# The first 128 columns of each weight chunk, 16 bytes ahead of the rest

## The chip, the core and the metric

The kernel runs on one core of one Trainium2 chip. The metric is the time of one execution on the device, in microseconds (us); lower is better. The core has a matrix engine (TensorE; PE in the profile, and PEld for its weight loads), VectorE (DVE), ScalarE (ACT), GpSimd (POOL) and SyncE (SP), which here issues the transfers from the chip's memory.

## What is computed

The reference runs two transformer blocks on 256 positions of width 1024, all in fp32, batch 1. The first adds 16 meta tokens in front (272 positions), then runs a gated feed-forward layer, a mixer with two kinds of attention, and a second feed-forward layer; the second block runs a convolution and a retention mixer, cross attention to 256 memory rows, and a squared-ReLU layer. Nearly all work is products of an activation with a weight matrix that is read once:

```python
def swiglu(h, w_in, w_out):
    gu = h @ w_in
    gate, up = jnp.split(gu, 2, axis=-1)
    return (jax.nn.silu(gate) * up) @ w_out

def first_block(...):
    h = jnp.concatenate([pad, meta, x], axis=1)
    for l in range(DEPTH):
        h = h + 0.5 * swiglu(rms_norm(h, ffn1_norm[l]), ffn1_w_in[l], ffn1_w_out[l])
        h = h + token_mixer(rms_norm(h, mix_norm[l]), ...)
        h = h + 0.5 * swiglu(rms_norm(h, ffn2_norm[l]), ffn2_w_in[l], ffn2_w_out[l])
    return h[:, BLOCK:]

def sq_relu_mlp(h, up_w, down_w):
    return jnp.square(jax.nn.relu(h @ up_w)) @ down_w
```

## The kernel before

**Layout.** Activations lie with features on the 128 partitions and positions along the row: 272 positions up to the mixer, 256 afterwards. A weight matrix is cut into blocks of 128 rows by 128 columns. One block is the stationary operand of a matmul, and 272 or 256 activation columns are the moving operand.

**Three matmuls for one product.** TensorE takes rounded fp32 (fp32r) here. Every weight and every activation is split in a high part, which is the rounded value, and a low part, which is the rest. `mm3` (lines 512 to 515) makes one product of three matmuls: weight high by activation high (L513), weight high by activation low (L514), weight low by activation high (L515). Each has a weight load of its own. There are 2360 such triples.

**Chunks of weights.** `_plan` lists all weights in the order of use and packs them into 164 chunks of at most 2048 columns, 16 blocks in most. `_Weights` carries each through three steps: `load` (L302) fetches a chunk into one of three `raw` buffers; `_high` (L319) writes the high part by ScalarE, in pieces of 1024 columns (256 in the first chunk); `piece` (L335) subtracts on VectorE and so writes the low part. `get` hands a block's two parts to the matmuls. The pools hold three chunks of high and of low parts, which the chunks take in turn.

**Where the parts lie.** `_part` takes a tile of 2048 + 64 fp32 columns and leaves the first `SHIFT` = 16 columns, 64 bytes, unused. Blocks follow each other without gaps, so every full block starts 64 bytes behind a multiple of 128 bytes; the activation tiles start on such multiples. The one exception is the chunk that begins with eight blocks of 8 columns (`fa`, the forget gate): there the blocks start in steps of 32 bytes.

**Order.** The program is written under a manual schedule: each engine runs its instructions in program order. `step` first splits what the product needs (`W.split`), then issues the matmuls, then the work on the results of the product before, interleaved with pieces for the chunks ahead. A chunk's load is issued when the low part of the chunk three before it is done. In the second mixer `beside` places convolution taps (L1045, VectorE) next to the pieces; `convolve(1e9)` issues what is left of them ahead of the mean over the convolution (L1269).

Of the kernel before, what the change touches and what calls it, by code (L numbers as in the profile page):

```python
# [10 lines left out]
F32 = mybir.dt.float32  # L11
F32R = mybir.dt.float32r
I32 = mybir.dt.int32
AF = mybir.ActivationFunctionType
ALU = mybir.AluOpType
AX = mybir.AxisListType

P = 128
# [6 lines left out]
XP = 320  # L25
LINE = 64
SHIFT = 16
DFF = 2816
MF = DFF // P
DFF2 = 4096  # L30
# [4 lines left out]
CH = 2048  # L35
# [7 lines left out]
def _plan():  # L43
# [7 lines left out]
    def pairs(tag, name, ms, per=2, base=0):  # L51
        ms = list(ms)
        for i in range(0, len(ms), per):
            blocks = []
            for m in ms[i : i + per]:
                blocks += tiles(tag, name, m, range(KD), base + m * P)
            chunks.append(blocks)

    def glu(tag, name, ms, off_g, off_u):
        for m in ms:  # L60
            blocks = []
            for k in range(KD):
                blocks.append(((tag + "g", m, k), name, k, off_g + m * P, P))
                blocks.append(((tag + "u", m, k), name, k, off_u + m * P, P))
            chunks.append(blocks)

    def down(tag, name, kt, per):
        for m in range(KD):
            for k0 in range(0, kt, per):
                chunks.append(tiles(tag, name, m, range(k0, min(k0 + per, kt)), m * P))  # L70

    glu("f1", "ffn1_w_in", range(MF), 0, DFF)
    down("d1", "ffn1_w_out", MF, 11)
# [18 lines left out]
    pairs("wo", "w_out", range(KD))  # L92
    glu("f2", "ffn2_w_in", range(MF), 0, DFF)
    down("d2", "ffn2_w_out", MF, 11)
# [180 lines left out]
class _Weights:  # L275
# [2 lines left out]

    def __init__(self, nc, pool, ws):
        self.nc, self.pool, self.ws = nc, pool, ws  # L280
        _, self.where, self.start, self.ends, self.total = _plan()
        self.raw, self.hi, self.lo = {}, {}, {}
        self.loaded = 0
        self.c, self.o = 0, 0
        self.begun = []
        self.done = 0
        self.used = 0
        self.free = 0
        self.beside = None
# [16 lines left out]
    def _part(self, tag, c):  # L306


        t = self.pool.tile([P, CH + LINE], F32R, tag=tag, bufs=3, name=f"{tag}{c}")
        return t[:, SHIFT : SHIFT + CH]  # L310

    def _high(self, n):
        c, a = self.c, self.o
        at, size = self.start[c]
        if a == 0:
            self.hi[c] = self._part("hi", c)
            self.lo[c] = self._part("lo", c)
        b = min(a + n, size)
        self.nc.scalar.activation(self.hi[c][:, a:b], self.raw[c][:, a:b], AF.Copy)  # L319
        self.begun.append((c, a, b))  # L320
        self.c, self.o = (c + 1, 0) if b == size else (c, b)

    def piece(self, to, n=1024):


        if to is None or self.done >= to or self.done >= self.total:
            return False
        while sum(self.start[self.free]) <= self.used:
            self.free += 1
        while len(self.begun) < 2 and self.c < min(len(self.start), self.free + 3):  # L330
            self._high(n)
        c, a, b = self.begun.pop(0)
        if self.beside:
            self.beside((b - a) / 1024)
        self.nc.vector.tensor_tensor(self.lo[c][:, a:b], self.raw[c][:, a:b], self.hi[c][:, a:b].bitcast(F32),  # L335
                                     op=ALU.subtract)
        self.done = self.start[c][0] + b
        if b == self.start[c][1]:
            self.load()
        return True  # L340
# [16 lines left out]
    def get(self, key):  # L357
        c, off, n = self.where[key]
        self.used = max(self.used, self.start[c][0] + off + n)
        return self.hi[c][:, off : off + n], self.lo[c][:, off : off + n]  # L360


LATER = object()
# [1242 lines left out]
```

## Time and profile before

| | |
|---|---|
| median of 3 runs | 982.52 us (981.97 to 982.52) |
| the profiled execution | 983.64 us |
| its span, first to last instruction | 981.6 us |
| PE busy | 965.1 us, 98% of the span, 7667 matmuls |
| VectorE busy | 675.4 us, 69% |
| ScalarE busy | 537.5 us, 55% |
| high parts (L319) and low parts (L335) | 321.8 us and 373.4 us, 334 pieces each |
| mean granted TensorE clock | 0.998 |
| transfers | 169 MB, mean 172 GB/s |

Times inside the trace count from the start of the span. A matmul's duration is longer than the distance to the next one, since they are pipelined: how many start in a stretch of time says how fast the engine goes. A count of instructions in a stretch takes in those that lie across its edges.

### The profile page before, as it was taken

To read this page: it belongs to the slowest core of one execution; us is meant where nothing else is said; L and a number is where in the kernel's file an instruction comes from. 1 tells how busy PE (TensorE), PEld (TensorE's weight loads), DVE (VectorE), ACT (ScalarE), POOL (GpSimd) and SP (SyncE) were. 2 spreads that over 40 slices of the span, in tenths; PEclk is the share of its full clock that TensorE was granted. 3 is DMA by queue.
4 is the path that set the end of the run, shared out by engine and by line. 5 is a ranking of instruction groups with operands and counts; after the bars stand their busy time and mean duration, and the time that the engine had idled before them with its cause. 6 is when DMAs were issued, how large, how long until landed. Compare 5 with 4: busy or idle time off the path is not lost.

```text
span 981.6 us, 18397 instructions
## 1 busy us (share of the span) xinstructions
PE 965.1 (98%) x7667; PEld 935.2 (95%) x7667; DVE 675.4 (69%) x1232; ACT 537.5 (55%) x927; POOL 9.9 (1%) x15
## 2 busy tenths in 40 slices
PE   7999999999999999999999999999999999999996
PEld 7999999999989899999999999889899999999996
DVE  5686656657875758677666657999976677675552
ACT  6545444456574656666454447556484566554441
POOL 0000000020000000000000000000000000000000
PEclk9999999999999999999999999999999999999999
DMA  8674526554523225554544656443544256555431
GB/s 298 191 264 172 173 92 233 191 185 138 173 94 123 96 99 214 215 215 173 194 166 157 209 191 235 168 155 138 202 159 155 86 182 221 199 194 194 173 128 43
DMA packets 31363, 169.05 MB, mean 172 GB/s; under 512 B 5144, under 2 KB 8864, under 8 KB 14640
## 3 DMA queue, kind: packets, MB, share of 16 engines
q1 hardware_dynamic: 30928, 167.34, 48.3%
q8 instruction: 60, 0.98, 0.4%
q10 hardware_dynamic: 288, 0.52, 0.1%
q14 instruction: 23, 0.19, 0.1%
q0 software_dynamic: 64, 0.01, 0.0%
HBM read 166.79 MB, written 1.07 MB: 171 GB/s over the span
## 4 chain that ended last, share of the span: by engine, by line
PE 75%; ACT 1%; DVE 1%; issue 0%; DVEq 0%
PE ps L513 14%; PE ps L515 14%; PE ps L514 14%; PE po L515 7%; PE po L514 7%; PE po L513 7%; PE ps L660 1%; PE ps L1007 1%; PE ps L1006 1%; PE ps L1005 1%; PE po L702 1%; PE ps L1308 1%; PE ps L1174 0%; PE po L1346 0%; PE po L716 0%; PE ps L766 0%
## 5 line engine op out<-in xcount | busy, mean ns | idle before, releaser
L335 DVE TENSOR_TENSOR lo<-raw,hi 128x1024 fp32r<-128x1024 f32 (+2 forms) x334 | 373.4, 1130 | 47.5 <-ACT hi L319 45.0
L319 ACT ACTIVATE hi<-raw 128x1024 fp32r<-128x1024 f32 (+2 forms) x334 | 321.8, 978 | 137.2 <-issue 43.8
L513 PE MATMUL ps<-XH,hi 128*128 128x256 f32 (+2 forms) x976 | 284.0, 291 | 5.7 <-ACT hi L319 4.3
L515 PE MATMUL ps<-XH,lo 128*128 128x256 f32 (+2 forms) x976 | 277.4, 284 | 0.8 <-DVE lo L335 0.8
L514 PE MATMUL ps<-XL,hi 128*128 128x256 f32 (+2 forms) x976 | 277.6, 284 | 0.0
L513 PEld LDWEIGHTS ps<-XH,hi 128*128 128x128 f32 (+1 forms) x976 | 184.4, 189 | 8.2 <-ACT hi L319 4.3
L514 PEld LDWEIGHTS ps<-XL,hi 128*128 128x128 f32 (+1 forms) x976 | 186.0, 191 | 1.8 <-DVE XL L527 0.5
L515 PEld LDWEIGHTS ps<-XH,lo 128*128 128x128 f32 (+1 forms) x976 | 184.3, 189 | 1.4 <-DVE lo L335 1.0
L513 PE MATMUL po<-XH,hi 128*128 128x256 f32 (+1 forms) x456 | 130.2, 285 | 0.2 <-DVE br L1071 0.2
L515 PE MATMUL po<-XH,lo 128*128 128x256 f32 (+1 forms) x456 | 129.0, 283 | 0.4 <-DVE lo L335 0.4
L514 PE MATMUL po<-XL,hi 128*128 128x256 f32 (+1 forms) x456 | 128.7, 282 | 0.0
L514 PEld LDWEIGHTS po<-XL,hi 128*128 128x128 f32 x456 | 86.7, 190 | 0.1
L515 PEld LDWEIGHTS po<-XH,lo 128*128 128x128 f32 x456 | 85.8, 188 | 0.6 <-DVE lo L335 0.6
L513 PEld LDWEIGHTS po<-XH,hi 128*128 128x128 f32 x456 | 85.7, 188 | 0.6 <-DVE br L1071 0.5
L624 ACT ACTIVATE s<-gr 128x272 f32<-128x272 f32 (+1 forms) x44 | 18.7, 426 | 108.5 <-DVE gr L622 108.5
L513 PE MATMUL ps<-AHf,hi 128*128 128x272 f32 (+1 forms) x220 | 62.4, 284 | 0.0
L514 PE MATMUL ps<-ALf,hi 128*128 128x272 f32 (+1 forms) x220 | 62.4, 284 | 0.0
L515 PE MATMUL ps<-AHf,lo 128*128 128x272 f32 (+1 forms) x220 | 62.4, 284 | 0.0
L1045 DVE SCALAR_TENSOR_TENSOR cv<-U,par,cv 128x256 f32<-128x256 f32 x120 | 50.1, 479 | 0.2 <-ACT cv L1078 0.2
L622 DVE TENSOR_TENSOR gr<-ps,r 128x272 f32<-128x272 f32 (+1 forms) x28 | 12.1, 434 | 48.4 <-PE ps L515 42.1
L513 PE MATMUL ps<-AHm,hi 128*128 128x256 f32 x160 | 45.0, 281 | 0.0
L514 PE MATMUL ps<-ALm,hi 128*128 128x256 f32 x160 | 45.0, 281 | 0.0
(385 smaller groups left out, 1827.8 us busy)
## 6 DMA issues: line engine op xcount, KB each, us to landing
raw<-in_ws_dram SPq DMA_DIRECT2D x128, 1024.0 KB, 4.8
raw<-in_ws_dram SPq DMA_DIRECT2D x32, 704.0 KB, 4.2
raw<-in_ws_dram SPq DMA_DIRECT2D x3, 512.0 KB, 5.6
dec<-in_dec_dram SPq DMA_DIRECT2D x1, 1536.0 KB, 6.4
BM<-drow SPq DMA_DIRECT2D x2, 512.0 KB, 5.7
memraw<-in_mt_dram SPq DMA_DIRECT2D x1, 1024.0 KB, 7.0
hA<-in_xt_dram SPq DMA_DIRECT2D x3, 273.0 KB, 6.0
raw<-in_ws_dram SPq DMA_DIRECT2D x3, 256.0 KB, 6.7
```

Of the source, the lines that this page charges most:

```text
L319: self.nc.scalar.activation(self.hi[c][:, a:b], self.raw[c][:, a:b], AF.Copy)
L335: self.nc.vector.tensor_tensor(self.lo[c][:, a:b], self.raw[c][:, a:b], self.hi[c][:, a:b].bitcast(F32), op=ALU.subtract)
L513: T.matmul(o, w[0], x[0], start=start, stop=False)
L514: T.matmul(o, w[0], x[1], start=False, stop=False)
L515: T.matmul(o, w[1], x[0], start=False, stop=stop)
L622: V.tensor_tensor(gr, g[:, :n], r[0][:, :n], op=ALU.mult)
L624: S.activation(s, gr, AF.Silu)
L660: T.matmul(ps[:, at : at + n], lhs, rhs, start=True, stop=True)
L702: T.matmul(o, st["v"](h, 0), pt[:, :SEQ], start=t % 2 == 0, stop=False)
L1005: T.matmul(ps[i], xh[:, t], wh, start=k == 0, stop=False)
L1006: T.matmul(ps[i], xl[:, t], wh, start=False, stop=False)
L1045: V.scalar_tensor_tensor(cv[:, m], U[:, m, j : j + SEQ], prm("cw", m * 31 + j), cv[:, m], op0=ALU.mult, op1=ALU.add)
```

## The change

The first block of a chunk's high part and of its low part is put 12 columns (`LEAD`, 48 bytes) behind the start of the tile; the rest of the chunk stays at 16 columns (64 bytes). So the first block moves 16 bytes towards the tile's start, and 16 bytes are left free between it and the second. This holds for the 157 chunks whose first block is 128 columns wide; the other seven (`fa`, and the six chunks of blocks of 512 columns for `rv` and `xv`) stay as they are. Since one instruction can't write across the gap, the first piece of a chunk is written by two instructions on ScalarE and by two on VectorE, 128 columns and the other 896 (in the first two chunks 128 and 128). Nothing is changed in the transfers, the tiles' sizes and places, the blocks' order or the matmuls' order.

```diff
+LEAD = 12
...
+        self.lead = [blocks[0][4] if blocks[0][4] == P else 0 for blocks in chunks]
...
     def _part(self, tag, c):
-        t = self.pool.tile([P, CH + LINE], F32R, tag=tag, bufs=3, name=f"{tag}{c}")
-        return t[:, SHIFT : SHIFT + CH]
+        return self.pool.tile([P, CH + LINE], F32R, tag=tag, bufs=3, name=f"{tag}{c}")
+
+    def _cols(self, t, c, a, b):
+        at = LEAD if b <= self.lead[c] else SHIFT
+        return t[:, at + a : at + b]
+
+    def _sides(self, c, a, b):
+        n = self.lead[c]
+        return [(a, n), (n, b)] if a < n < b else [(a, b)]
...
         b = min(a + n, size)
-        self.nc.scalar.activation(self.hi[c][:, a:b], self.raw[c][:, a:b], AF.Copy)
+        for i, j in self._sides(c, a, b):
+            self.nc.scalar.activation(self._cols(self.hi[c], c, i, j), self.raw[c][:, i:j], AF.Copy)
...
-        self.nc.vector.tensor_tensor(self.lo[c][:, a:b], self.raw[c][:, a:b], self.hi[c][:, a:b].bitcast(F32),
-                                     op=ALU.subtract)
+        for i, j in self._sides(c, a, b):
+            self.nc.vector.tensor_tensor(self._cols(self.lo[c], c, i, j), self.raw[c][:, i:j],
+                                         self._cols(self.hi[c], c, i, j).bitcast(F32), op=ALU.subtract)
...
     def get(self, key):
...
-        return self.hi[c][:, off : off + n], self.lo[c][:, off : off + n]
+        return self._cols(self.hi[c], c, off, off + n), self._cols(self.lo[c], c, off, off + n)
```

VectorE in the second feed-forward layer, before, around the low part of chunk 73 (`lo` and `hi` are the chunk's parts, `gr`, `a` and `ALf` belong to the results of the product before):

```order
L622 TENSOR_TENSOR gr_5351<-po_5230,r_4879 128x256
L335 TENSOR_TENSOR lo_5290<-raw_5222,hi_5289 128x1024
L626 TENSOR_TENSOR a_5353<-ps_5231,s_5352 128x256
L335 TENSOR_TENSOR lo_5290<-raw_5222,hi_5289 128x1024
L525 TENSOR_TENSOR ALf_4761<-a_5353,AHf_4760 128x256
```

The same place after the change:

```order
L636 TENSOR_TENSOR gr_5569<-ps_5446,r_5012 128x256
L349 TENSOR_TENSOR lo_5507<-raw_5438,hi_5506 128x128
L349 TENSOR_TENSOR lo_5507<-raw_5438,hi_5506 128x896
L640 TENSOR_TENSOR a_5571<-ps_5447,s_5570 128x256
L349 TENSOR_TENSOR lo_5507<-raw_5438,hi_5506 128x1024
L539 TENSOR_TENSOR ALf_4891<-a_5571,AHf_4890 128x256
```

The first of the two pieces is now two instructions; what stands around it keeps its order, and ScalarE shows the same.

PE at the start of the same chunk, before, with the semaphores that a matmul waits for:

```order
L513 MATMUL ps_5372<-XH,hi_5289 128x256 [waits Activation_49]
L514 MATMUL ps_5372<-XL,hi_5289 128x256
L515 MATMUL ps_5372<-XH,lo_5290 128x256 [waits DVE_49]
L513 MATMUL ps_5373<-XH,hi_5289 128x256
L514 MATMUL ps_5373<-XL,hi_5289 128x256
L515 MATMUL ps_5373<-XH,lo_5290 128x256
```

And after:

```order
L527 MATMUL po_5592<-XH,hi_5506 128x256 [waits Activation_49]
L528 MATMUL po_5592<-XL,hi_5506 128x256
L529 MATMUL po_5592<-XH,lo_5507 128x256 [waits DVE_49]
L527 MATMUL po_5593<-XH,hi_5506 128x256 [waits Activation_49]
L528 MATMUL po_5593<-XL,hi_5506 128x256
L529 MATMUL po_5593<-XH,lo_5507 128x256 [waits DVE_49]
```

The matmuls and their order are the same. The first three read the block that was moved, and the second block now has two waits of its own, on the instruction that wrote it.

## Rows read from the trace of the kernel before

**Rows 1.** Page, part 1: busy time, share of the span and instructions of each engine

```profile
PE 965.1 (98%) x7667; PEld 935.2 (95%) x7667; DVE 675.4 (69%) x1232; ACT 537.5 (55%) x927; POOL 9.9 (1%) x15
```

**Rows 2.** Waits of PE: who waited for whom, us in total, times, longest

```profile
PE ps L513 <- ACT hi L319: 4.3, 1, 4.3
```

**Rows 3.** Stretches: edges and length, busy time and count by engine, clock, DMA share

```profile
core 0: us, PE busy (x) PEld busy (x) DVE busy (x) ACT busy (x) POOL busy (x), PEclk, DMA share, GB/s
358.00:410.00 52.00, 52.00 (x461) 52.00 (x461) 42.49 (x75) 34.08 (x60) 0.00 (x0) 1.00 0.55 199
412.00:588.00 176.00, 176.00 (x1497) 176.00 (x1496) 115.11 (x181) 91.48 (x149) 1.11 (x2) 1.00 0.53 183
...
721.00:738.00 17.00, 17.00 (x152) 17.00 (x151) 14.84 (x26) 13.25 (x23) 0.00 (x0) 1.00 0.53 186
...
774.00:799.00 25.00, 25.00 (x223) 25.00 (x222) 20.57 (x34) 15.56 (x26) 0.00 (x0) 1.00 0.48 166
801.00:971.00 170.00, 170.00 (x1446) 170.00 (x1445) 101.75 (x143) 84.44 (x136) 0.00 (x0) 1.00 0.45 164
32.00:210.00 178.00, 178.00 (x1445) 178.00 (x1444) 112.73 (x182) 82.61 (x127) 1.36 (x1) 1.00 0.55 185
```

**Rows 4.** Groups by form, 358 to 410 us: matmuls, then weight loads

```profile
L513 PE MATMUL ps<-XH,hi 128*128 128x256 f32 x30 | 8.3, 276 | 0.0
...
L514 PEld LDWEIGHTS ps<-XL,hi 128*128 128x128 f32 x30 | 5.6, 188 | 0.0
```

**Rows 5.** The same groups, 412 to 588 us

```profile
L513 PE MATMUL ps<-XH,hi 128*128 128x256 f32 x200 | 56.2, 281 | 0.0
...
L514 PEld LDWEIGHTS ps<-XL,hi 128*128 128x128 f32 x200 | 38.4, 192 | 0.0
```

**Rows 6.** PE in order of time around 411 us: start, duration (us)

```profile
409.50 0.28 PE L515 MATMUL ps<-XH,lo 128*128 128x256 f32 x1
...
410.86 0.28 PE L515 MATMUL ps<-XH,lo 128*128 128x256 f32 x1
410.98 0.59 PE L562 MATMUL ps<-acc,c 128*128 128x256 f32 x2
...
411.53 0.28 PE L514 MATMUL po<-XL,hi 128*128 128x256 f32 x1
...
412.71 0.28 PE L515 MATMUL po<-XH,lo 128*128 128x256 f32 x1
```

**Rows 7.** PE in order of time around 618 us

```profile
617.71 0.70 PE L1088 MATMUL ps<-br,cst 128*128 128x256 f32 x2
...
618.37 0.28 PE L514 MATMUL ps<-XL,hi 128*128 128x256 f32 x1
...
619.40 0.28 PE L514 MATMUL ps<-XL,hi 128*128 128x256 f32 x1
```

**Rows 8.** Groups by form over the whole span: the pieces of high and low parts

```profile
L319 ACT ACTIVATE hi<-raw 128x1024 fp32r<-128x1024 f32 x291 | 303.0, 1050 | 132.7 <-issue 43.8 <-PE ps L514 36.7 <-PE po L514 29.0
...
L319 ACT ACTIVATE hi<-raw 128x384 fp32r<-128x384 f32 x32 | 16.3, 509 | 0.0
```

**Rows 9.** The same for VectorE

```profile
L335 DVE TENSOR_TENSOR lo<-raw,hi 128x1024 fp32r<-128x1024 f32 x291 | 352.6, 1219 | 47.2 <-ACT hi L319 44.7
...
L335 DVE TENSOR_TENSOR lo<-raw,hi 128x384 fp32r<-128x384 f32 x32 | 17.6, 551 | 0.0
```

**Rows 10.** Stretch of the second mixer, columns as in rows 3

```profile
617.00:704.00 87.00, 86.85 (x564) 76.61 (x564) 85.79 (x165) 46.22 (x71) 0.00 (x0) 1.00 0.43 156
```

**Rows 11.** End of the convolution on VectorE, and the matmuls that read it

```profile
705.48 0.47 DVE L1045 SCALAR_TENSOR_TENSOR cv<-U,par,cv 128x256 f32<-128x256 f32 x1
...
707.09 1.89 PE L1269 MATMUL ps<-cv,cst 128*128 128x256 f32 x8
```

**Rows 12.** Groups by form, 237.4 to 240.1 us: weight blocks of 8 columns

```profile
L514 PE MATMUL ps<-XL,hi 128*8 128x272 f32 x8 | 2.3, 286 | 0.0
```

**Rows 13.** The same for full blocks of this form, 32 to 210 us

```profile
L514 PE MATMUL ps<-XL,hi 128*128 128x272 f32 x185 | 53.1, 287 | 0.0
```

More of the change, by code (lines that the diff above doesn't have):

```diff
@@ L280, in __init__ @@
         self.nc, self.pool, self.ws = nc, pool, ws
-        _, self.where, self.start, self.ends, self.total = _plan()
+        chunks, self.where, self.start, self.ends, self.total = _plan()
+        self.lead = [blocks[0][4] if blocks[0][4] == P else 0 for blocks in chunks]
         self.raw, self.hi, self.lo = {}, {}, {}
```

## The prediction

> **What bounds the kernel now.** The first view is the page's list of engines: TensorE is busy 965.1 us of a span of 981.6 us, VectorE 69%, ScalarE 55% [rows 1]. The second is the list of TensorE's waits: the longest is the 4.3 us before the first weights are there, and that is the only wait for a high part [rows 2]. So the time is the number of matmuls times the distance from one to the next, and the third view is the one that matters: how many matmuls start in a stretch without a stop. I take (length + one duration) / count, since a count includes the matmuls on the edges.
>
> All the matmuls with 256 moving columns do the same work, in the same layout, at a granted clock of 1.00 [rows 3]. Still there are two paces. From 358 to 410 us: (52.00 + 0.276) / 461 = 113.4 ns. From 412 to 588 us: (176.00 + 0.281) / 1497 = 117.8 ns. From 721 to 738 us it is 113.7, from 774 to 799 us 113.4, and from 801 to 971 us (170.00 + 0.28) / 1446 = 117.8 ns. The groups by form agree: a matmul lasts 276 ns in the one stretch [rows 4] and 281 in the other, where the weight load of L514 also lasts 192 ns instead of 188 [rows 5]. Other engines don't explain it: the quick stretch from 358 us has the denser VectorE (42.49 of 52 us, against 115.11 of 176) and more transfers (199 against 183 GB/s) [rows 3]. I read this as two self-sustaining rhythms between weight loads and matmuls. What changes the rhythm is a break: matmuls start every 1.36 us / 12 = 113 ns up to 410.86 us, then come the plain fp32 matmuls of L562, and from 411.53 us ten steps take 1.18 us, 118 ns each [rows 6]. At 618 us the fp32 matmuls of L1088 are such a break too, and the restart comes out quick: nine steps in 1.03 us, 114 ns each [rows 7]. The slow rhythm then lasts 176 and 170 us, through chunk after chunk, because nothing in a chunk disturbs it.
>
> **Part 1, the moved block on TensorE.** No matmul is added or reordered. The two weight parts of the first block, read by three loads per moving tile group, start 16 bytes elsewhere in a 128-byte frame. No row of before shows a block at 48 bytes. The nearest is the chunk with blocks of 8 columns, in steps of 32 bytes: 286 ns a matmul [rows 12], against 287 for full blocks in that part of the kernel [rows 13]. So as a steady price the address is worth 0 to 1 ns on 272 columns, in a rhythm that there is always 123.4 ns ((178.00 + 0.286) / 1445, last line of rows 3); I put the chunks of that part at nothing.
>
> With 256 columns two rhythms exist, and there the one odd weight load at each chunk's start can act as a small break. I choose this: a kick repeated at every chunk leaves the rhythm that it leaves least easily, and this is the quick one, since the quick one is also the one with no stretched load [rows 4, 5]. That is an inference from the two groups, not a thing the trace shows. The gain is then 117.76 - 113.4 = 4.36 ns for each matmul of the slow stretches: 1497 x 4.36 = 6.5 us from 412 to 588 us; 1446 less one chunk's some 24 to be kicked in, x 4.36 = 6.2 us from 801 to 971 us. Together -12.7 us.
>
> The kick has a price. The restart at 618 us took 1.03 us for nine steps that at 113.4 ns take 1.02, so 10 ns; as ends I take 0 and 20 ns. Some 100 of the moved chunks lie in the part with 256 columns: +1.0 us (0 to 2.0).
>
> **Part 2, the pieces on ScalarE and VectorE.** 157 first pieces become two instructions each. ScalarE takes 1050 ns for 1024 columns and 509 for 384 [rows 8]: 0.845 ns a column and 184 ns fixed. VectorE takes 1219 and 551 [rows 9]: 1.044 ns a column and 150 ns fixed. So the second instruction adds up to 157 x 0.184 = 29 us on ScalarE and 157 x 0.150 = 24 us on VectorE. Both engines are idle for far more (45% and 31% of the span, [rows 1]), and the pieces run ahead of TensorE, so nearly all of it is hidden. If that cover were gone it would show as waits of L513 and L515 on L319 and L335, of which the first has one now [rows 2].
>
> The exception is the second mixer. From 617 to 704 us VectorE is busy 85.79 of 87 us [rows 10]. What ends this stretch is the convolution: its last tap ends at 705.48 + 0.47 = 705.95 us, and the matmuls of L1269 that read it start at 707.09 us, 1.14 us later [rows 11]. Some 9 chunks are prepared there: 9 x 0.150 = 1.35 us, or 1.66 us if a short piece costs VectorE the 184 ns that it costs ScalarE, against those 1.14 us. I take +0.2 us (0 to 0.5). For the same reason I count no gain from a quicker TensorE there: it would only meet VectorE earlier.
>
> **Part 3, the added waits.** The second block of a chunk waits for its own instruction on each engine. Queued behind it on TensorE is the rest of the chunk. It is met when it comes: the first piece of a chunk is finished whole chunks ahead, apart from the start, where the first 128 columns come a little sooner than the 256 of before. Nothing.
>
> **The sum.** -12.7 + 1.0 + 0.2 = -11.5 us. The profiled execution took 983.64 us, its span 981.6 and 2.04 us around it; this gives 972.1 us by it. It stands 1.1 us above the median of 982.52, so against the median 971.0 us. Its own range is 969 to 975: the kick at 0 or 20 ns, and a tenth to a fifth of the slow matmuls left slow.
>
> **Rivals.** *The kick throws both ways.* If each chunk's start picks a rhythm anew, half of the matmuls are slow. In the five shown stretches there are 1497 + 1446 = 2943 slow and 461 + 152 + 223 = 836 quick; half of 3779 is 1890, so 1053 x 4.36 = -4.6 us, with +1.2 for price and VectorE: 979 us (974 to 981). For it: breaks before the change end both ways [rows 6, 7].
>
> *The 16 bytes do nothing.* The rhythm then goes on through the chunk's start, and what is left is the extra instructions: 983 us (982 to 984). For it: the groups of 8-column blocks [rows 12, 13] show no effect of the offset. The Trainium skill, page "SBUF — State Buffer", section "Door 1: The DMA port swizzle", gives 16-byte cachelines, and its section "Who interferes with whom" says "PE and ACT never wait on anyone." By these a block at 48 bytes covers as many lines as one at 64, and nothing of this change could reach the matmuls: 983 us. The trace bears that out for the lack of an effect of VectorE and transfers, but it gives no account of two paces for the same operands [rows 4, 5], so a rule without a pace cannot settle it.
>
> *Slower: the kick throws the quick rhythm out.* Place: the stretches from 358, 721 and 774 us. If the odd load puts the rhythm in the 118 ns form, 836 x 4.36 = +3.6 us, and the moved first blocks each cost 10 to 20 ns without a return, 157 x 0.010 to 0.020 = 1.6 to 3.1 us, with +0.2 for VectorE: 988 to 989.5 us (985 to 991). It decides when matmuls behind the first moved block in 358 to 410 us go at 118 ns. For it: the slow form holds 2943 of 3779 of these matmuls, so it may be the one that is easier to fall into.
>
> **How the numbers follow.** The kick into the quick form has 0.48, since a load out of step is the only new thing on the bound engine, and the form without a stretched load is the one that I take it to end in. Both ways 0.12, nothing 0.18, slower 0.22. About 0.2% or 2 us is what a measurement of this kernel can tell from no change. Faster is then 0.48 + 0.12 - 0.01 for the upper edge of the second case = 0.59, same 0.18, slower 0.23. The range reaches over the first three cases, 0.78, and into the lower part of the last, with a little left out under 969: 968 to 987.
>
> **What would show it.** In the changed trace from 412 to 588 us and from 801 to 971 us (each shifted by what was gained) the count should give 113 to 114 ns, the groups 276 ns instead of 281 and 188 ns for the load of L514. VectorE should have 157 instructions more, some 20 us, and no new wait on L319 or L335 among TensorE's. The matmul at 707 us should still follow the convolution within about 1 us. I am wrong if the slow stretches stay at 118 ns (nothing), if quick and slow change from chunk to chunk (both ways), or if 358 to 410 us goes at 118 ns (slower). I am also wrong if the 272-column part leaves 123.4 ns: it holds some 44 moved chunks, and 1 ns on every one of its 1445 matmuls from 32 to 210 us alone would be 1.4 us.

## Result and the profile after

The changed kernel takes 970.88 us (median of 4 runs, 970.52 to 971.35), against 982.52 us (median of 4 runs, 981.97 to 982.94); the ratio is 0.9881, 95% interval 0.9868 to 0.9893. The forecast was 971.0 us.

The profiled execution has a span of 968.8 us, 12.8 us less than before. Engines, from the page of the changed kernel:

```profile
PE 951.9 (98%) x7667; PEld 922.0 (95%) x7667; DVE 684.6 (71%) x1389; ACT 550.7 (57%) x1084; POOL 9.9 (1%) x15
```

Against [rows 1]: the same 7667 matmuls, TensorE's busy time is 13.2 us shorter, and VectorE and ScalarE have 157 instructions more each. The waits of TensorE in the changed kernel, who waited for whom, us in total, times, longest:

```profile
PE ps L527 <- ACT hi L332: 4.2, 1, 4.2
...
PE ps L529 <- DVE lo L349: 1.2, 2, 0.7
...
PE po L529 <- DVE lo L349: 0.5, 1, 0.5
```

L527 to L529 are what L513 to L515 were; as in [rows 2] the only wait for a high part is the one at the start. The waits for a low part are three, 1.7 us together; L515 had two before:

```profile
PE ps L515 <- DVE lo L335: 0.8, 1, 0.8
...
PE po L515 <- DVE lo L335: 0.4, 1, 0.4
```

None of these waits became shorter by more than 0.1 us, so the 12.8 us lie in how fast the matmuls follow each other. Stretches of the changed kernel, columns as in [rows 3]:

```profile
358.00:410.00 52.00, 52.00 (x458) 52.00 (x456) 42.68 (x83) 34.38 (x68) 0.00 (x0) 1.00 0.55 201
412.00:576.00 164.00, 164.00 (x1445) 164.00 (x1444) 116.34 (x215) 94.24 (x183) 0.00 (x0) 1.00 0.56 194
...
797.00:957.00 160.00, 160.00 (x1410) 160.00 (x1410) 100.56 (x168) 84.65 (x160) 0.00 (x0) 1.00 0.48 172
32.00:210.00 178.00, 178.00 (x1443) 178.00 (x1443) 115.28 (x219) 85.54 (x162) 1.62 (x1) 1.00 0.55 186
```

With (length + one duration) / count: from 412 to 576 us 164.276 / 1445 = 113.7 ns, where 117.8 stood, and from 797 to 957 us 160.276 / 1410 = 113.7, where 117.8 stood. From 358 to 410 us, quick before, it is 52.276 / 458 = 114.1 against 113.4. The part with 272 columns hardly moves: 1443 matmuls instead of 1445, 123.6 ns instead of 123.4. The groups of the stretch from 412 to 576 us (busy us, mean ns) have the numbers that [rows 4] had for the quick pace, and no longer those of [rows 5]:

```profile
L527 PE MATMUL ps<-XH,hi 128*128 128x256 f32 x200 | 55.3, 276 | 0.0
...
L528 PEld LDWEIGHTS ps<-XL,hi 128*128 128x128 f32 x200 | 37.6, 188 | 0.0
```

The first matmuls of chunks 66, 102 and 134, before:

```profile
411.22 0.47 PE L513 MATMUL po<-XH,hi 128*128 128x256 f32 x1
...
586.66 0.28 PE L513 MATMUL po<-XH,hi 128*128 128x256 f32 x1
...
802.77 0.28 PE L513 MATMUL po<-XH,hi 128*128 128x256 f32 x1
```

And after:

```profile
411.15 0.47 PE L527 MATMUL po<-XH,hi 128*128 128x256 f32 x1
...
580.47 0.28 PE L527 MATMUL po<-XH,hi 128*128 128x256 f32 x1
...
795.90 0.28 PE L527 MATMUL po<-XH,hi 128*128 128x256 f32 x1
```

By these starts the 12.8 us come from four stretches:

| stretch | before, us | after, us | difference |
|---|---|---|---|
| start to chunk 66 | 411.22 | 411.15 | -0.07 |
| chunk 66 to 102 (second feed-forward layer) | 175.44 | 169.32 | -6.12 |
| chunk 102 to 134 (mixer and cross attention) | 216.11 | 215.43 | -0.68 |
| chunk 134 to the end (last layer) | 178.83 | 172.90 | -5.93 |

### The profile page after: what moved, and what is told of

The parts are those of the page before. It is cut to its first block, busy times and chain, and to the rows that moved or that the text cites. A ratio compares the mean times of both kernels' runs of the same rounds, so it can differ in the third digit from the quotient of the medians.

```text
span 968.8 us, 18713 instructions
## 1 busy us (share of the span) xinstructions
PE 951.9 (98%) x7667; PEld 922.0 (95%) x7667; DVE 684.6 (71%) x1389; ACT 550.7 (57%) x1084; POOL 9.9 (1%) x15
## 4 chain that ended last, share of the span: by engine, by line
PE 95%; ACT 2%; DVE 1%; DMA 1%; SPq 1%; issue 0%; DVEq 0%; ACTq 0%
PE ps L527 18%; PE ps L529 18%; PE ps L528 18%; PE po L529 10%; PE po L528 10%; PE po L527 10%; PE ps L674 1%; PE ps L1021 1%; PE ps L1020 1%; PE ps L1019 1%; PE po L716 1%; DMA raw<-in_ws_dram 1%; PE ps L1322 1%; DVE lo L349 0%; PE ps L1188 0%; PE po L730 0%
## 5 line engine op out<-in xcount | busy, mean ns | idle before, releaser
L349 DVE TENSOR_TENSOR lo<-raw,hi 128x128 fp32r<-128x128 f32 (+4 forms) x491 | 387.2, 817 | 39.0 <-ACT hi L332 38.8
L332 ACT ACTIVATE hi<-raw 128x128 fp32r<-128x128 f32 (+4 forms) x491 | 336.6, 726 | 127.3 <-issue 43.0
L527 PE MATMUL ps<-XH,hi 128*128 128x256 f32 (+2 forms) x976 | 281.9, 289 | 5.6 <-ACT hi L332 4.2
L529 PE MATMUL ps<-XH,lo 128*128 128x256 f32 (+2 forms) x976 | 275.4, 282 | 1.2 <-DVE lo L349 1.2
L527 PEld LDWEIGHTS ps<-XH,hi 128*128 128x128 f32 (+1 forms) x976 | 183.9, 188 | 8.2 <-ACT hi L332 4.2
L529 PEld LDWEIGHTS ps<-XH,lo 128*128 128x128 f32 (+1 forms) x976 | 183.8, 188 | 2.0 <-DVE lo L349 1.6
L528 PEld LDWEIGHTS ps<-XL,hi 128*128 128x128 f32 (+1 forms) x976 | 184.0, 188 | 1.8 <-DVE XL L541 0.5
L527 PE MATMUL po<-XH,hi 128*128 128x256 f32 (+1 forms) x456 | 129.2, 283 | 0.2 <-DVE br L1085 0.2
L529 PE MATMUL po<-XH,lo 128*128 128x256 f32 (+1 forms) x456 | 127.9, 280 | 0.5 <-DVE lo L349 0.5
L529 PEld LDWEIGHTS po<-XH,lo 128*128 128x128 f32 x456 | 85.8, 188 | 0.7 <-DVE lo L349 0.7
L527 PEld LDWEIGHTS po<-XH,hi 128*128 128x128 f32 x456 | 85.7, 188 | 0.6 <-DVE br L1085 0.4
L527 PE MATMUL ps<-AHf,hi 128*128 128x272 f32 (+1 forms) x220 | 62.0, 282 | 0.0
L529 PE MATMUL ps<-AHf,lo 128*128 128x272 f32 (+1 forms) x220 | 61.9, 281 | 0.0
L527 PE MATMUL ps<-AHm,hi 128*128 128x256 f32 x160 | 44.2, 276 | 0.0
L529 PE MATMUL ps<-AHm,lo 128*128 128x256 f32 x160 | 44.2, 276 | 0.0
```

Of the source, the lines that this page charges most:

```text
L332: self.nc.scalar.activation(self._cols(self.hi[c], c, i, j), self.raw[c][:, i:j], AF.Copy)
L349: self.nc.vector.tensor_tensor(self._cols(self.lo[c], c, i, j), self.raw[c][:, i:j], self._cols(self.hi[c], c, i, j).bitcast(F32), op=ALU. ...
L527: T.matmul(o, w[0], x[0], start=start, stop=False)
L528: T.matmul(o, w[0], x[1], start=False, stop=False)
L529: T.matmul(o, w[1], x[0], start=False, stop=stop)
```

## Experiments

A **triple** is the three matmuls of one product; I take its length from the starts of the matmuls in the trace. In the quick pace it is 340 ns, in the slow one 353 to 354 ns. The question in each experiment is what the triples behind a chunk's start do.

**1. The two instructions without the move.**

```diff
-LEAD = 12
+LEAD = 16
```

> The changed kernel with LEAD = 16: the pieces are still written by two instructions and the second block still has its own waits, but no block is moved. Theory (the moved block is what turns the pace of the matmuls): the long stretches go at 117.8 ns as before, and the time is 982 to 984 us; the 157 extra instructions each on ScalarE and VectorE are worth 0 to 1 us. Rival (the extra waits at the second block, or the later start of the second piece, turn the pace): 970 to 972 us, with 113.4 ns in the long stretches.

983.35 us, ratio 1.0002 (0.9992 to 1.0012). The counts in the stretches of [rows 3] are those of before:

```profile
358.00:410.00 52.00, 52.00 (x461) 52.00 (x460) 42.55 (x83) 34.65 (x69) 0.00 (x0) 1.00 0.55 203
412.00:588.00 176.00, 176.00 (x1497) 176.00 (x1496) 117.74 (x218) 94.57 (x184) 1.70 (x2) 1.00 0.54 182
...
801.00:971.00 170.00, 170.00 (x1446) 170.00 (x1445) 102.99 (x171) 85.96 (x162) 0.00 (x0) 1.00 0.46 162
```

461, 1497 and 1446, with PE at 100% of each. The extra pieces and the extra waits neither turn the pace nor cost anything that can be measured. All of the gain belongs to the move.

**2. The whole chunk at 48 bytes**, made from the kernel before.

```diff
-SHIFT = 16
+SHIFT = 12
```

> The kernel before with SHIFT = 12: whole chunks start at 48 bytes, no gap between the first block and the second, no extra instructions. Theory (the step between two offsets turns the pace, the offset itself does nothing): nothing within a chunk stands out, each stretch keeps the pace in which it restarts, 975 to 985 us, with whole stretches of hundreds of matmuls at one pace and no dear triple at a chunk's start. Rival (48 bytes is a better place for a weight block than 64): 113.4 ns in all stretches with 256 columns from start to end, 968 to 970 us, below the changed kernel since no chunk start costs anything.

990.8 us, ratio 1.0080 (1.0065 to 1.0095): slower, which neither side expected.

```profile
358.00:410.00 52.00, 52.00 (x444) 52.00 (x443) 42.74 (x75) 34.44 (x60) 0.00 (x0) 1.00 0.53 188
414.00:588.00 174.00, 174.00 (x1480) 174.00 (x1479) 114.08 (x179) 91.72 (x148) 0.00 (x0) 1.00 0.54 183
...
32.00:210.00 178.00, 178.00 (x1433) 178.00 (x1432) 112.34 (x183) 82.29 (x125) 0.47 (x1) 1.00 0.55 185
```

52.28 / 444 = 117.7 ns and 174.28 / 1480 = 117.8 ns: the stretch that was quick is slow too, and from 358 us to the end no triple takes the 340 ns of the quick pace. At 272 columns it is 178.288 / 1433 = 124.4 ns against 123.4. So 48 bytes is no better place: in the changed kernel the first block itself gains nothing from it, the blocks behind it do. And the steady offset does have a price: at 272 columns 1.0 ns, the upper end of the prediction's 0 to 1 ns, and at 256 columns the quick pace. The Trainium skill, page "SBUF — State Buffer", section "Door 1: The DMA port swizzle", gives 16-byte cachelines, by which blocks at 48 and at 64 bytes cover the same number of lines; here they differ by 1 ns a matmul at 272 columns and by 4.4 ns at 256, so the number of lines alone does not set the pace.

**3. Five moved blocks.** Only the chunks 76, 80, 84, 148 and 152 have a moved first block.

```diff
-        self.lead = [blocks[0][4] if blocks[0][4] == P else 0 for blocks in chunks]
+        self.lead = [blocks[0][4] if blocks[0][4] == P and c in (76, 80, 84, 148, 152) else 0 for c, blocks in enumerate(chunks)]
```

> The changed kernel with the first block moved in five chunks only: 76, 80 and 84 in the stretch from 412 to 588 us, 148 and 152 in the one from 801 to 971 us. Theory (a moved block ends the slow pace with an even chance or so, and never the quick one): the pace is 117.8 ns up to one of these chunks and 113.4 ns from there to the stretch's end. If 76 and 148 do it: 10 chunks of 412 to 588 us and 14 of 801 to 971 us stay slow, 16 triples of 13.2 ns each, 5.1 of the 12.7 us are not gained, and the time is about 975 us; if none of them does it, 982.5; each chunk later costs 0.8 us more. Rival (the moved block makes only its own chunk quicker and has to come again in each): five chunks of 0.2 us, 981.5 us, with the slow pace back in the chunk behind each.

974.96 us, ratio 0.9919 (0.9904 to 0.9934), as the theory had it for the case that the first of each group does it. Chunk 76 begins at 466.64 us, chunk 148 at 876.36 us; the stretches ahead of each and behind it:

```profile
412.00:466.00 54.00, 54.00 (x461) 54.00 (x460) 40.42 (x66) 33.67 (x58) 0.00 (x0) 1.00 0.52 180
468.00:576.00 108.00, 108.00 (x954) 107.96 (x954) 70.92 (x113) 55.30 (x90) 0.00 (x0) 1.00 0.57 193
801.00:876.00 75.00, 75.00 (x639) 75.00 (x638) 55.36 (x86) 45.73 (x84) 0.00 (x0) 1.00 0.56 197
878.00:960.00 82.00, 82.00 (x726) 82.00 (x725) 41.77 (x50) 34.33 (x43) 0.00 (x0) 1.00 0.42 148
```

Ahead 54.28 / 461 = 117.8 and 75.28 / 639 = 117.8 ns; behind 108.28 / 954 = 113.5 and 82.28 / 726 = 113.3 ns. The turn itself, PE in order of time (start, duration in us):

```profile
465.70 0.28 PE L528 MATMUL ps<-XL,hi 128*128 128x256 f32 x1
...
466.64 0.28 PE L527 MATMUL ps<-XH,hi 128*128 128x256 f32 x1
466.76 0.28 PE L528 MATMUL ps<-XL,hi 128*128 128x256 f32 x1
...
467.47 0.28 PE L528 MATMUL ps<-XL,hi 128*128 128x256 f32 x1
...
468.38 0.28 PE L527 MATMUL ps<-XH,hi 128*128 128x256 f32 x1
```

Nine steps up to 466.76 us take 1.06 us (118 ns), six more to 467.47 take 0.71 (118), and the eight from 467.47 to 468.38 take 0.91 (114). The first two triples of chunk 76 are still slow, and from the third on the pace is quick. It stays so through the 25 chunks to the stretch's end, 23 of them without a moved block. So the rival by which each chunk needs a moved block of its own falls.

**4. One part alone.** `_cols` gives 48 bytes to one of the two parts only; for the high part:

```diff
-        at = LEAD if b <= self.lead[c] else SHIFT
+        at = LEAD if b <= self.lead[c] and t is self.hi[c] else SHIFT
```

> The changed kernel with only the high part's first block moved, the low part's first block stays at 64 bytes; instructions and waits as in the changed kernel. In the changed kernel a chunk's first triple takes 352 ns and the others 340. Theory A (any load that is out of step acts): the long stretches go at 113.4 ns, time 970 to 971.5 us, the first triple dearer by up to 12 ns. Rival B (the step from the low part to the high part of the first triple, or the low part alone, acts): long stretches at 117.8 ns, 982 to 984 us.

973.09 us, ratio 0.9899 (0.9884 to 0.9914). For the low part (`self.lo[c]`):

> The changed kernel with only the low part's first block moved, the high part's first block stays at 64 bytes; instructions and waits as in the changed kernel. Theory A (any load out of step acts, the high part alone did: 973.1 us with first triples of 372 and 346 ns): the long stretches go at 113.4 ns, 970 to 974 us. Rival B (only the two loads of the high part act, which stand one behind the other): 117.8 ns in the long stretches, 982 to 985 us.

973.04 us, ratio 0.9898 (0.9883 to 0.9913). Both times are far from rival B's, but the first lies above theory A's 970 to 971.5 us: each kernel is some 2 us behind the changed one, for two reasons. The stretch from 358 to 410 us, high part alone, then low part alone:

```profile
358.00:410.00 52.00, 52.00 (x457) 52.00 (x456) 43.62 (x85) 35.27 (x69) 0.00 (x0) 1.00 0.54 193
```

```profile
358.00:410.00 52.00, 52.00 (x444) 52.00 (x443) 42.77 (x83) 34.47 (x68) 0.00 (x0) 1.00 0.53 194
```

The high part alone turned all nine slow chunks that it met, but costs 40 ns at each quick one; 81 of these, 27 ns dearer than in the changed kernel, are 2.2 us. The low part alone costs 13.5 ns, but turned two of fourteen: this stretch came in slow and went through ten moved chunks without a turn (117.7 ns). So for the low part theory A holds in the time more than in the turns.

What gave the low part its quick long stretch from 412 us is a break. The fp32 matmuls of L576 stand directly ahead of chunk 66. Behind them, low part alone:

```profile
412.80 0.47 PE L527 MATMUL po<-XH,hi 128*128 128x256 f32 x1
...
413.69 0.28 PE L527 MATMUL po<-XH,hi 128*128 128x256 f32 x1
...
414.71 0.28 PE L527 MATMUL po<-XH,hi 128*128 128x256 f32 x1
```

High part alone:

```profile
412.10 0.47 PE L527 MATMUL po<-XH,hi 128*128 128x256 f32 x1
...
412.99 0.28 PE L527 MATMUL po<-XH,hi 128*128 128x256 f32 x1
...
414.05 0.28 PE L527 MATMUL po<-XH,hi 128*128 128x256 f32 x1
```

From the third triple on, nine steps take 1.02 us (113 ns) with the low part moved and 1.06 us (118 ns) with the high part moved; there it was chunk 67 that turned the pace. The same holds in all profiles: chunk 66 came out of this break quick in the five in which its low part is moved (the changed kernel twice, low part alone, and the two kernels of 5) and slow in the eight in which it is not. So the changed kernel won its first long stretch at the break itself, by its low part as these two kernels show, and not by a turn out of the slow pace.

**5. A step of 64 bytes, and one of 32.**

```diff
-LEAD = 12
+LEAD = 0
```

> The changed kernel with LEAD = 0: the first block starts at the tile's start, 64 bytes ahead of its place of before instead of 16. Theory (a step in the offset turns the pace, whatever its size): long stretches at 113.4 ns, 969 to 975 us. Rival (it takes a block at 48 bytes, where the run with whole chunks at 48 bytes knew the slow pace only): the first triples take 340 or 353 ns like the others, the long stretches stay at 117.8 ns, 982 to 984 us.

987.05 us, ratio 1.0041 (1.0027 to 1.0055): neither, but slower than before. PE around the start of chunk 67 at 418.33 us:

```profile
417.31 0.28 PE L527 MATMUL po<-XH,hi 128*128 128x256 f32 x1
...
418.33 0.28 PE L527 MATMUL po<-XH,hi 128*128 128x256 f32 x1
...
419.75 0.28 PE L527 MATMUL po<-XH,hi 128*128 128x256 f32 x1
```

Nine steps ahead of it take 1.02 us (113 ns), the twelve behind it 1.42 us (118 ns). Chunk 66 had come out of its break quick, and the moved block of chunk 67 ended that; so it went at all seven chunks that began quick, and none of the 83 that began in the slow pace turned. This is the prediction's slower rival, by its mechanism, with a larger step. With LEAD = 8:

> The changed kernel with LEAD = 8: the first block 32 bytes ahead of the others instead of 16. So far the step by 16 bytes turned slow to quick and never quick to slow, and the step by 64 bytes turned quick to slow at all seven chunks that were quick. Theory E (a small step turns to quick, only a large one to slow): the long stretches at 113.4 ns, 970 to 974 us. Rival F (48 bytes is the one place that turns to quick, all others turn to slow): the long stretches and the one from 358 to 410 us at 117.8 ns, 984 to 988 us. If it does neither, 982 to 984 us.

971.72 us, ratio 0.9888 (0.9872 to 0.9905), as theory E: 83 quick starts stayed quick, six of seven chunks that began in the slow pace turned, at 20 ns each in the quick pace.

**6. Another disturbance, without an address.** In the kernel before, the first two matmuls of the first triple change places, in the same five chunks as in 3.

```diff
+        self.turn = off == 0 and c in (76, 80, 84, 148, 152)
...
-        T.matmul(o, w[0], x[0], start=start, stop=False)
-        T.matmul(o, w[0], x[1], start=False, stop=False)
+        i, j = (1, 0) if W.turn else (0, 1)
+        T.matmul(o, w[0], x[i], start=start, stop=False)
+        T.matmul(o, w[0], x[j], start=False, stop=False)
```

> The kernel before, no block moved, but in the first triple of the chunks 76, 80, 84, 148 and 152 the high part meets the activations' low part first and their high part second. Theory C (any triple out of step ends the slow pace, an address is not needed): the pace turns from 117.8 to 113.4 ns at one of 76, 80, 84 and at one of 148, 152; 975 us if the first of each does it, up to 980 if the last. Rival D (it takes the address): no turn, 982 to 983.5 us.

983.36 us, ratio 1.0003 (0.9994 to 1.0013), no turn: rival D.

```profile
412.00:588.00 176.00, 176.00 (x1497) 176.00 (x1496) 115.04 (x181) 91.57 (x148) 0.78 (x2) 1.00 0.53 183
801.00:971.00 170.00, 170.00 (x1446) 170.00 (x1445) 101.75 (x143) 85.22 (x138) 0.00 (x0) 1.00 0.47 166
```

Both counts are those of before to the matmul, and the changed triples take 353 ns like their neighbours. At these five chunks another order of the moving operand was no disturbance; another address of the weights, in 3, turned the pace at 76 and at 148.

**7. Only where it is needed.** The high part's first block, moved in nine chunks in or behind which the slow pace sets in; `_cols` is that of the high part in 4.

```diff
+KICK = (57, 67, 103, 113, 114, 121, 125, 126, 134)
...
-        self.lead = [blocks[0][4] if blocks[0][4] == P else 0 for blocks in chunks]
+        self.lead = [blocks[0][4] if blocks[0][4] == P and c in KICK else 0 for c, blocks in enumerate(chunks)]
```

> The high part's first block moved in nine chunks only: 57, 67, 103, 113, 114, 121, 125, 126 and 134, the ones in or behind which the slow pace sets in after a break. Theory (the quick pace once found needs no help, and each chunk start of the changed kernel costs 12 ns in it): the long stretches at 113.4 ns, some 90 dear first triples less than in the changed kernel, 90 x 12.5 = 1.1 us, and the extra pieces gone: 969.3 to 970.3 us, against 970.9 of the changed kernel. Rival (the quick pace falls back to the slow one by itself or at small waits, and the repeated push holds it): 972 to 980 us.

969.42 us, ratio 0.9861 (0.9846 to 0.9876). Stretches:

```profile
358.00:410.00 52.00, 52.00 (x461) 52.00 (x460) 42.24 (x74) 33.77 (x60) 0.00 (x0) 1.00 0.55 202
418.00:576.00 158.00, 158.00 (x1395) 157.96 (x1395) 109.77 (x172) 86.30 (x140) 0.00 (x0) 1.00 0.58 199
797.00:957.00 160.00, 160.00 (x1415) 160.00 (x1414) 97.79 (x139) 82.49 (x131) 0.00 (x0) 1.00 0.48 172
```

One moved block at 417 us, and 158.28 / 1395 = 113.5 ns to the end of the layer; from 797 to 957 us five matmuls more than in the changed kernel in the same time. It was timed once more beside the changed kernel, on one chip:

> The changed kernel as it is, beside the next kernel on the same chip: 970.9 us as in its first timing, ratio to the kernel before 0.988.

> The kernel with the high part's first block moved in nine chunks, beside the changed kernel on the same chip. Theory (a chunk start with a moved block costs 13 ns in the quick pace, and nine are enough): 1.0 to 1.6 us less than the changed kernel, 969.3 to 969.9 us. Rival (the difference seen in its first timing was that of another chip or hour): the same as the changed kernel within 0.4 us.

970.48 us for the changed kernel (ratio 0.9878, 0.9863 to 0.9893) and 969.41 us for this one (0.9872, 0.9857 to 0.9887). The medians are 1.1 us apart, as worked out, but the intervals overlap; the gain over the changed kernel rests on the counts in the traces rather than on the times.

The chunk starts with 256 columns at which the pace ahead and behind can be read, by the step that was made there, the other blocks at 64 bytes (profiles of one kind together, so that the same chunk counts in several):

| step at the chunk's start | slow: turned | quick: fell | price in the quick pace |
|---|---|---|---|
| none (before, 1, 6) | 0 of 211 | 0 of 59 | 0 |
| none (the chunks left alone in 3, 7 twice) | 0 of 29 | 0 of 219 | 0 |
| both parts, 16 bytes (after twice, 3) | 9 of 13 | 0 of 172 | 13 ns |
| high part, 16 bytes (4, 7 twice) | 18 of 18 | 0 of 88 | 40 ns |
| low part, 16 bytes (4) | 2 of 14 | 0 of 76 | 13.5 ns |
| both, 32 bytes (5) | 6 of 7 | 0 of 83 | 20 ns |
| both, 64 bytes (5) | 0 of 83 | 7 of 7 | - |

## Why the prediction was right

**The two paces and what they are worth** held. The forecast put 6.5 and 6.2 us on the two long stretches, less some 10 ns at 36 and 29 chunk starts, so -6.1 and -5.9; they gave -6.12 and -5.93 us. Experiment 1 shows that nothing else of the change takes part, experiment 3 that one moved block is enough to turn a stretch, and the table that without one no pace ever changed at a chunk's start: the 176 and 170 us of slow pace were a state that lasted for want of a disturbance. The first of the two gains was made at the break ahead of chunk 66 (experiment 4), where the forecast had a chunk's start within the slow pace.

**That the medians meet the forecast within 0.1 us** is in part luck. By the spans of the profiled executions the gain is 12.8 us, 1.3 us more than the forecast's 11.5: the parts outside the two long stretches gave -0.75 us, where the sum had a loss of some 0.5. The medians differ by 11.6 us, since the profiled execution before stood 1.1 us above its median and the one after 0.3 us below.

**The direction** was an inference in the forecast, and only its result was right. "A kick leaves the rhythm that it leaves least easily, and this is the quick one" holds for 16 and 32 bytes, 0 of 419 quick starts fell, and is false for 64 bytes. Which form a push ends in depends on the step. Nothing in the trace of before could tell that, and the chance of 0.22 for the slower rival was what that ignorance was worth: it is the outcome of LEAD = 0. (In the sum of the chances 0.01 that was taken from faster went to slower, 0.23, without a reason.)

**The price of a kick** was put at 10 ns (0 to 20) from a restart after fp32 matmuls; it is 13 ns. It shows as a loss between the first matmuls of chunks 58 and 66, where both kernels go at the quick pace: 41.15 us against 41.05. With some 100 chunks the term is 1.3 instead of 1.0 us. The chunks with 272 columns, put at nothing, cost 7 ns each (the four triples around a start last 1487 ns instead of 1480), 0.3 us for 44 of them.

**The waits** were to stay as they were. One was added: a 0.4 us wait of L529 for a low part at 17 us. The prediction passed over the two that L515 had before.

**It does not turn every time**, which the forecast allowed for as a tenth to a fifth left slow: 9 of 13. A chunk that begins slow costs one chunk more, since the next one tries again; in the profiled run chunks 56, 113 and 125 were such.

**ScalarE and VectorE.** A short piece and its rest, from the groups by form of the changed kernel:

```profile
L349 DVE TENSOR_TENSOR lo<-raw,hi 128x896 fp32r<-128x896 f32 x155 | 168.4, 1086 | 13.8 <-ACT hi L332 13.6
...
L349 DVE TENSOR_TENSOR lo<-raw,hi 128x128 fp32r<-128x128 f32 x159 | 45.0, 284 | 21.6 <-ACT hi L332 21.5
```

1086 + 284 - 1219 = 151 ns more for each on VectorE [rows 9], as worked out (150). But VectorE's busy time grew by 9.2 us, not by the 24 us that 157 x 0.150 gave or the "some 20" of the last part: busy time counts overlapping instructions once. For the second mixer I had feared 0.2 us. The margin there did shrink, the last convolution tap and the matmuls that read it now being

```profile
699.19 0.48 DVE L1059 SCALAR_TENSOR_TENSOR cv<-U,par,cv 128x256 f32<-128x256 f32 x1
700.00 1.89 PE L1283 MATMUL ps<-cv,cst 128*128 128x256 f32 x8
```

0.33 us apart instead of the 1.14 of [rows 11], but it is not used up: no wait of L1283 is listed. Instead the mixer and cross attention gained 0.68 us, which the forecast had at nothing: 0.4 us of that is in four chunks with 512 moving columns (116 to 119), whose 32 triples take 687 ns instead of 700 once the chunk ahead of them hands them the quick pace.

**The rule that nothing can reach TensorE** ("PE and ACT never wait on anyone", the Trainium skill, page "SBUF — State Buffer", section "Who interferes with whom") stood behind the second rival. As far as other engines go the traces agree: in experiment 1 ScalarE and VectorE have 157 instructions more each, and the counts of matmuls are those of before. The rival fell all the same, since the addresses of TensorE's own weights change its pace.

**Still open** is what the two paces are inside the engine. The runs show that the quick one occurs with chunks at 64 bytes and was not seen with all of them at 48, that a different offset of one block is what turns the pace, and that 16 and 32 bytes turn it one way and 64 bytes the other. The size of the step and the place of the block (48, 32 and 0 bytes) changed together, so which of the two decides is not shown. Why 64 bytes turns the other way, why the low part alone turns the slow pace so seldom, and why it is the one that counts at the break ahead of chunk 66, was not found out.

## What to carry to other kernels

Where one engine is at 98% without waits, count how many equal instructions start in equal stretches: two paces for the same work are time to be had, although no wait shows it. If the pace changes only at breaks, look for the cheapest disturbance, place it once behind each break rather than everywhere, and test it in a few places first, since a slightly different one can do the reverse.

## What the runs showed of the hardware

- Matmuls with 128x128 fp32r weights and 256 moving columns, at a granted clock of 1.00, follow each other at 113.4 or at 117.8 ns; the pace lasts for more than a hundred us and changed at no undisturbed chunk start of 518.
- With all weight blocks at 48 instead of 64 bytes behind a multiple of 128 only the slow pace was seen, and with 272 columns 124.4 ns instead of 123.4.
- One weight block 16 bytes out of step costs 13 ns (both parts) to 40 ns (high part alone) in the quick pace. It ended the slow one at 9 of 13 starts (both parts), 18 of 18 (high part alone) and 2 of 14 (low part alone); 64 bytes out of step ended the quick one at 7 of 7.
- Directly behind one break, ahead of chunk 66, the pace came out quick in 5 of 5 profiles with the low part's first block moved and slow in 8 of 8 without.
